# A norm weight applied to weight pieces on GpSimd, and its RMS factor applied to the products, in a two-layer decoder kernel

## The chip, the cores and the metric

The kernel runs on one core of a Trainium2 chip. The metric is the device time of one execution in microseconds (us). A core has five engines with instruction queues of their own, which the profile calls PE (TensorE, the matrix engine; PEld is its loading of stationary operands), DVE (VectorE), ACT (ScalarE), POOL (GpSimd) and SP (SyncE, which here only issues DMAs). Each engine works off its queue in order and waits where an instruction's operands aren't there yet.

## The reference

The input is x, 512 tokens of 2048 features in float32. Two layers follow each other. Each normalizes its input, mixes it, normalizes the result and adds it to the residual stream:

```python
def rms_norm(x, w):
    xf = x.astype(jnp.float32)
    y = xf * lax.rsqrt(jnp.mean(xf * xf, axis=-1, keepdims=True) + EPS)
    return (y * w.astype(jnp.float32)).astype(x.dtype)
...
    for layer in range(DEPTH):
        h = rms_norm(x, norm_pre[layer])
        ...
        x = x + rms_norm(y, norm_post[layer])
```

The even layer (layer 1 in the text) has gated linear recurrence heads and a gated MLP. The odd layer (layer 2) is a latent attention; its head is what matters here:

```python
    z = h @ w_in
    cq, ckv, kpe, gate = split_sizes(z, [C_Q_RANK, C_KV_RANK, C_ROPE, C_WIDTH])
    q = (rms_norm(cq, q_norm) @ w_qb).reshape(bsz, T, C_HEADS, C_QK)
    kv = (rms_norm(ckv, kv_norm) @ w_kvb).reshape(bsz, T, C_HEADS, C_NOPE + C_V)
    ...
    return (o * jax.nn.silu(gate)) @ w_out
```

`w_in` of the odd layer is 2048 x 3136: 512 columns for cq, 512 for ckv, 64 for the rotary key kpe, 2048 for the gate. EPS is 1e-6.

## The kernel before

The 512 tokens are four tiles of 128 (NT = 4), the 2048 features 16 blocks of 128 (KD = 16). Every float32 product is made of three matmuls in a reduced float32 format: each operand is split into a high part (a cast) and a low part (the operand minus its high part), and high x high, high x low and low x high are summed in PSUM. `tok_steps` (L209 to L211) does so with the activations stationary and 128 tokens in the partitions of the output, `feat_steps` (L214 to L216) with the weights stationary and 128 features in the partitions.

**Weights** come in pieces of 128 x 1024 numbers (512 KB). `fetch` issues the DMA on SP (L150) into `raw`, which has three buffers. `wload` splits the piece: ACT casts it into `whi` (L168), DVE makes `wlo` (L169). `piece(n)` prepares up to piece n + 3 (AHEAD). The pieces follow each other in one list, `plan`. A "stack" piece (the rotary key) writes high and low parts side by side (L162, L163).

**Activations** of a layer's input projection stand in R: 16 feature blocks, each as a high and a low tile of 128 features x 512 tokens. To get there, a tile of 128 tokens x 2048 features is transposed on TensorE in four groups of 512 features (L297; four 128 x 128 transposes into one PSUM bank `tp`), and each group is split from PSUM into R by ACT (L279) and DVE (L280). There are two `tp` banks in turn, so the third transpose of a tile needs the bank that the first one's two splits have read.

**The border of the two layers.** Layer 1 ends with `out_proj` ("eo"): 2048 output features in chunks of 512, 512, 512, 256 and 256. The last chunk runs tile by tile: 48 matmuls per token tile, then `last_evac` for this tile: squares on ACT (L673), weight of the post-norm on DVE (L674), sum of squares (L679), RMS factor `yrs` on POOL (`rstd_of`, L271 and L272), and four residual adds on DVE (L683), each 128 x 512: Wa = Wa * yrs + residual. Then `finish0` stores the tile (L710, four DMAs) and starts `pre_norm` of layer 2 for it: squares on ACT (L286), sum on DVE (L288), factor `prs` on POOL, and, put off by some ticks, four steps of one scaling on DVE (L292: B = Wa * prs * weight row) and one transpose (L297) with its two splits. `tick()` counts pieces in the matmul loops; `at(DEFER + c // 2, ...)` places the steps that many ticks on, so that they fall between matmuls of the following work. Layer 2 then runs `low_rank("cq")` (eight pieces; the first four tile by tile), the rotary key (one piece), `low_rank("ckv")` (eight pieces) and the gate (`proj_feat` for eight chunks of four pieces; `gate_evac`, L790 to L793, makes silu of each PSUM bank). In `low_rank`, each output row is normalized again with a factor `lrs` over its 512 features.

What sets the order on each engine: the kernel's Python code emits instructions, and the framework's scheduler then puts them into the five in-order queues and places the semaphores. So the order is fixed before the kernel runs, and an instruction that waits holds up all that stand behind it in its queue.

Of the kernel before, what the change touches and what calls it, by code (L numbers as in the profile page):

```python
# [10 lines left out]
F32 = mybir.dt.float32  # L11
# [7 lines left out]
P = 128  # L19
T = 512  # L20
NT = T // P
D = 2048
# [22 lines left out]
def trunk_kernel(ctx, tc, x, positions, norm_pre, norm_post, ev_w_in, ev_lb_logits, ev_a_onorm,  # L45
# [17 lines left out]
    def tp_bank():  # L63
        return ptp.tile([P, 512], F32, name="tp", tag="tp")
# [25 lines left out]
    def row_bc(dst, src_row):  # L90
        nc.sync.dma_start(out=dst, in_=src_row.partition_broadcast(P))
# [12 lines left out]
    mhalf = const.tile([P, 8], F32, name="mhalf")  # L104
    nc.gpsimd.memset(mhalf, -0.5)

    pk = const.tile([18, P], F32, name="pk")
    nc.sync.dma_start(out=pk[0:16, :], in_=ev_lb_logits.rearrange("l (h p) -> (l h) p", p=P))
    nc.sync.dma_start(out=pk[16:17, :], in_=ev_a_onorm)
    nc.sync.dma_start(out=pk[17:18, :], in_=inv_freq)  # L110

    cols = const.tile([P, 18], F32, name="cols")
    lb = const.tile([P, 8], F32, name="lb")
    oml = const.tile([P, 8], F32, name="oml")

    def setup_cols():
        tp = tp_bank()
        nc.tensor.transpose(tp[:, 0:18], pk, ident[0:18, 0:18])
        nc.scalar.copy(cols, tp[:, 0:18])
        e = sm.tile([P, 4, 8], F32, name="lbt", bufs=1)  # L120
        l0, l1 = cols[:, 0:8], cols[:, 8:16]
        nc.vector.tensor_tensor(e[:, 0], l0, l1, ALU.max)
        nc.vector.tensor_tensor(e[:, 1], l0, e[:, 0], ALU.subtract)
        nc.vector.tensor_tensor(e[:, 2], l1, e[:, 0], ALU.subtract)
        nc.scalar.activation(e[:, 1:3], e[:, 1:3], AF.Exp)
        nc.vector.tensor_tensor(e[:, 3], e[:, 1], e[:, 2], ALU.add)
        nc.vector.reciprocal(e[:, 3], e[:, 3])
        nc.vector.tensor_tensor(lb, e[:, 1], e[:, 3], ALU.mult)
        nc.vector.tensor_scalar(oml, lb, -1.0, 1.0, ALU.mult, ALU.add)
# [2 lines left out]
    def wview(w):  # L132
        return w.rearrange("(k p) c -> p k c", p=P)

    plan, ready, issued = [], {}, [0]
    AHEAD = 3
    DEFER = 6

    def plan_chunk(wv, c0, ncol, nk_all, nk, cuts=None):
        first = len(plan)  # L140
        for k in range(0, nk_all, nk):
            plan.append((wv[:, k:k + nk, c0:c0 + ncol], nk, ncol, cuts))
        return first

# [8 lines left out]
    def wload(i):  # L153
        _, nk, nco, cuts = plan[i]
        n = nk * nco
        if i not in fetched:
            fetch(i)
        raw = fetched.pop(i)
        if cuts == "stack":
            rv = raw[:, 0:n].rearrange("p (k c) -> p k c", k=nk)  # L160
            st = low_rank_act()[:, 8:12, :].rearrange("p a (k c) -> p (a k) c", c=P)
            nc.scalar.copy(st[:, :, 0:64], rv)  # L162
            nc.vector.tensor_tensor(st[:, :, 64:128], rv, st[:, :, 0:64].bitcast(F32), ALU.subtract)  # L163
            return st, None
# [104 lines left out]
    def rstd_of(ss, n, ncols, name, bufs=2):  # L269
        r = sm.tile([P, ncols], F32, name=name, bufs=bufs)  # L270
        nc.gpsimd.tensor_scalar(r, ss, 1.0 / n, EPS, ALU.mult, ALU.add)  # L271
        nc.gpsimd.tensor_tensor(r, r, mhalf[:, 0:ncols], ALU.pow)  # L272
        return r
# [62 lines left out]

    plan_out("eo", ev_w_out[0])
    for c in range(2):
        pl["cq", c] = plan_chunk(ow, CQ + 256 * c, 256, KD, 4)
    pl["kpe"] = plan_chunk(ow, KPE, 64, KD, KD, "stack")  # L340
    pl["ckv"] = plan_chunk(ow, CKV, 512, KD, 2)
    for c in range(8):
        pl["gate", c] = plan_chunk(ow, GATE + 256 * c, 256, KD, 4)
    for p in range(8):
        pl["q", p] = plan_chunk(qv, p * 384, 384, 4, 2, cuts_q)
        pl["kv", p] = plan_chunk(kvv, p * 512, 512, 4, 2)
# [307 lines left out]
    def out_proj(Wy, name, wpost_row, resid_t, junk, finish, early=KD, hook=None):  # L654
# [47 lines left out]
        proj_tok(pl[name, 3], 256, r_act, KD, lambda i, ps: evac(i, ps, 1536, 3))  # L702
        proj_tok(pl[name, 4], 256, r_act, KD, last_evac, tile_major=True)

    def finish0(i, ch):
        if i == 0:
            for c in range(4):
                row_bc(B[:, 4 + c, :], norm_pre[1, c * 512:(c + 1) * 512])
        for c in range(4):
            nc.sync.dma_start(out=x1_t[i][:, c * 512:(c + 1) * 512], in_=ch[c])  # L710
        pre_norm(i, ch, [B[:, 4 + c, :] for c in range(4)],
                 [B[:, 8 + 4 * (i % 2) + c, :] for c in range(4)], G[:, 8, :], DEFER)

    out_proj(W, "eo", norm_post[0], x_t, G[:, 8, :], finish0)

# [6 lines left out]
    def low_rank(name, wbc, rows, dst, first):  # L722
        ss = sm.tile([P, 4, 2], F32, name="lss")

        def evac(i, ps, half):
            n = ps.shape[-1]
            nc.scalar.activation(G[:, 8, 0:n], ps, AF.Square, accum_out=ss[:, i, half:half + 1])
            nc.vector.tensor_tensor(rows[i][:, half * 256:half * 256 + n], ps,
                                    wbc[:, half * 256:half * 256 + n], ALU.mult)

# [5 lines left out]
        else:  # L736
            proj_tok(pl[name], 512, r_act, KD, lambda i, ps: evac(i, ps, 0))
            s1 = ss[:, :, 0]
        r = rstd_of(s1, 512, 4, "lrs")
        def flip(i):  # L740
            tp = tp_bank()
            for j in range(4):
# [16 lines left out]
    def rope_half(dst, src_ps, src_sb, sw, n):  # L759
# [4 lines left out]
        nc.gpsimd.tensor_tensor(sw[0:n], sw[0:n], sinT[0:n], ALU.mult)  # L764
        nc.vector.tensor_tensor(dst[0:n], dst[0:n], sw[0:n], ALU.add)


    kps = mm_bank()
    stk, _ = piece(pl["kpe"])
# [244 lines left out]
```

## Time and profile before

| | us |
|---|---|
| median of 3 runs | 1601.81 (1601.14 to 1602.43) |
| the profiled execution | 1602.72 |
| its span, first to last instruction | 1601.0 |
| DVE, residual adds of layer 1 (L683), one of 128 x 512 | 0.747 (median of 16) |
| mean granted TensorE clock | 0.998 |

One execution was profiled, and it lies 0.9 us above the median of the runs. Durations are taken from it. In rows of the timeline the first number is the start in us from the start of the span, the second the duration; a bracket gives the idle time of the engine ahead of the instruction and what ended it. In rows of groups stand busy time, mean ns of one instruction, and idle time ahead with what ended most of it. `out<-in` gives the tiles by name, `raw`, `whi`, `wlo` for weights, `Wa` for the residual stream of layer 1's end, `B` for scaled rows, `R` for split activations, `G` for the residual loaded from memory.

### The profile page before, as it was taken

What the parts mean: (1) busy time and instruction counts of PE and PEld (TensorE: products, weight loads), DVE (VectorE), ACT (ScalarE), POOL (GpSimd) and SP (SyncE); (2) the same over time, 40 slices, a digit from 0 to 9 for tenths busy, and PEclk for the clock granted to TensorE, in tenths of its full rate; (3) what the DMA queues carried; (4) which work ended last, traced back from release to release, by engine and by line L of the source; (5) the groups of instructions that cost most, each with busy time, mean ns of one, the idle gap of its engine ahead of it and who ended that gap; (6) DMA issues with size and microseconds to landing.
All of it is one profiled execution on the core that took longest, in us unless ns stands there. A gap on an engine that the chain in (4) does not pass through costs nothing. (4 is left out here: it accounts for less than half of the span.)

```text
span 1601.0 us, 20791 instructions
## 1 busy us (share of the span) xinstructions
PE 1574.7 (98%) x8417; PEld 1359.2 (85%) x8417; DVE 752.5 (47%) x1346; ACT 534.6 (33%) x928; POOL 96.6 (6%) x145
## 2 busy tenths in 40 slices
PE   6999999999999999999999999999999999999997
PEld 5888888898888888888889988888889888988887
DVE  7653455535444224352225743232266767762224
ACT  6422322222222222232224433222265555642221
POOL 1000000000014004000001000000000000000000
PEclk9999999999999999999999999999999999999999
DMA  6432232223333333343325523333221221233224
GB/s 214 123 93 79 86 98 80 80 79 99 92 100 119 100 102 94 99 145 100 111 93 160 168 69 105 92 93 99 86 74 56 70 60 60 93 106 105 93 93 158
DMA packets 124299, 161.03 MB, mean 101 GB/s; under 512 B 7830, under 2 KB 86696, under 8 KB 124200
## 3 DMA queue, kind: packets, MB, share of 16 engines
q1 hardware_dynamic: 124204, 159.71, 32.1%
q8 instruction: 66, 1.08, 0.3%
q14 instruction: 29, 0.24, 0.0%
HBM read 151.30 MB, written 8.39 MB: 100 GB/s over the span
## 5 line engine op out<-in xcount | busy, mean ns | idle before, releaser
L169 DVE TENSOR_TENSOR wlo<-raw,whi 128x1024 fp32r<-128x1024 f32 x240 | 297.0, 1238 | 635.9 <-ACT whi L168 619.9
L168 ACT CAST whi<-raw 128x1024 fp32r<-128x1024 f32 x240 | 252.2, 1052 | 768.3 <-PE mm L211 338.9
L209 PE MATMUL mm<-whi,R 128*128 128x512 f32 (+1 forms) x1152 | 397.5, 345 | 0.0
L210 PE MATMUL mm<-wlo,R 128*128 128x512 f32 (+1 forms) x1152 | 395.8, 344 | 1.2 <-DVE wlo L169 1.2
L211 PE MATMUL mm<-whi,R 128*128 128x512 f32 (+1 forms) x1152 | 395.8, 344 | 0.0
L214 PE MATMUL mm<-R,whi 128*128 128x512 f32 x832 | 326.0, 392 | 0.0
L216 PE MATMUL mm<-R,wlo 128*128 128x512 f32 x832 | 324.0, 389 | 0.0
L215 PE MATMUL mm<-R,whi 128*128 128x512 f32 x832 | 323.9, 389 | 0.0
L210 PEld LDWEIGHTS mm<-wlo,R 128*128 128x128 f32 x1152 | 219.2, 190 | 26.3 <-DVE wlo L169 1.7
L211 PEld LDWEIGHTS mm<-whi,R 128*128 128x128 f32 x1152 | 219.1, 190 | 25.1
L209 PEld LDWEIGHTS mm<-whi,R 128*128 128x128 f32 x1152 | 219.2, 190 | 24.7 <-ACT R L279 0.2
L216 PEld LDWEIGHTS mm<-R,wlo 128*128 128x128 f32 x832 | 156.2, 188 | 32.8
L214 PEld LDWEIGHTS mm<-R,whi 128*128 128x128 f32 x832 | 156.2, 188 | 32.1
L215 PEld LDWEIGHTS mm<-R,whi 128*128 128x128 f32 x832 | 156.3, 188 | 31.8
L214 PE MATMUL mm<-Wc,whi 128*128 128x512 f32 x160 | 62.9, 393 | 0.0
L216 PE MATMUL mm<-Wc,wlo 128*128 128x512 f32 x160 | 62.6, 391 | 0.0
L215 PE MATMUL mm<-Wc,whi 128*128 128x512 f32 x160 | 62.4, 390 | 0.0
L280 DVE TENSOR_TENSOR R<-mm,R 128x512 fp32r<-128x512 f32 x48 | 32.9, 686 | 27.5 <-ACT R L279 27.5
L280 DVE TENSOR_TENSOR R<-tp,R 128x512 fp32r<-128x512 f32 x64 | 42.1, 684 | 4.0 <-ACT R L279 3.7
L279 ACT CAST R<-tp 128x512 fp32r<-128x512 f32 x64 | 35.9, 587 | 18.9 <-PE tp L297 17.0
L904 ACT ACTIVATE G<-sc,nm 128x512 f32<-128x512 f32 (+2 forms) x48 | 26.1, 546 | 41.2 <-DVE nm L903 41.2
L279 ACT CAST R<-mm 128x512 fp32r<-128x512 f32 x48 | 28.2, 587 | 31.8 <-PE mm L211 18.3
(245 smaller groups left out, 1653.7 us busy)
## 6 DMA issues: line engine op xcount, KB each, us to landing
raw<-in_ev_w_in_dram SPq DMA_DIRECT2D x112, 512.0 KB, 3.6
raw<-in_od_w_in_dram SPq DMA_DIRECT2D x49, 512.0 KB, 3.8
raw<-in_ev_w_out_dram SPq DMA_DIRECT2D x32, 512.0 KB, 3.6
raw<-in_od_w_out_dram SPq DMA_DIRECT2D x32, 512.0 KB, 3.5
raw<-in_od_w_kvb_dram SPq DMA_DIRECT2D x16, 512.0 KB, 3.5
raw<-in_od_w_qb_dram SPq DMA_DIRECT2D x16, 384.0 KB, 3.3
Wa<-in_x_dram SPq DMA_DIRECT2D x16, 256.0 KB, 5.7
G<-in_x_dram SPq DMA_DIRECT2D x16, 256.0 KB, 5.0
```

The lines of the kernel that those rows point to most:

```text
L168: nc.scalar.copy(hi[:, 0:n], raw[:, 0:n])
L169: nc.vector.tensor_tensor(lo[:, 0:n], raw[:, 0:n], hi[:, 0:n].bitcast(F32), ALU.subtract)
L209: nc.tensor.matmul(o, hh[:, sl], wh, start=first, stop=False, skip_group_check=True)
L210: nc.tensor.matmul(o, hh[:, sl], wl, start=False, stop=False, skip_group_check=True)
L211: nc.tensor.matmul(o, hl[:, sl], wh, start=False, stop=last, skip_group_check=True)
L214: nc.tensor.matmul(ps, hi, hh, start=first, stop=False)
L215: nc.tensor.matmul(ps, hi, hl, start=False, stop=False)
L216: nc.tensor.matmul(ps, lo, hh, start=False, stop=last)
L279: nc.scalar.copy(dst_hi, src)
L280: nc.vector.tensor_tensor(dst_lo, src, dst_hi.bitcast(F32), ALU.subtract)
L904: nc.scalar.activation(pv[j], sp[j], AF.Exp, bias=nm[:, j:j + 1], scale=C_SCALE, accum_out=su[:, j:j + 1])
```

## The change

The pre-norm of layer 2 is h = x * rn * w, with a factor rn for each token and a weight w for each feature. Before, both are applied to x ahead of its transposes. The change applies w to the rows of `w_in` and rn to the products.

- The 16 feature blocks of `norm_pre[1]` are brought into `cols` as 16 columns (one more small DMA at the start; the transpose in `setup_cols` takes 34 rows in place of 18).
- The 49 pieces of `w_in` (cq 8, kpe 1, ckv 8, gate 32) are marked in `norm_k`. In `wload`, POOL multiplies such a piece in place in `raw`, before the cast and the subtraction, by the column of its feature block, broadcast along the row.
- The four row broadcasts of `norm_pre[1]` and the 16 scalings (L292) of layer 2 are gone. The transposes take the residual stream Wa itself, one tick earlier (DEFER is 5).
- `factor()` makes rn of a tile three ticks after its first transposes: squares on ACT, a sum on DVE, three small operations on POOL. It also keeps EPS * (mean square + EPS), which takes the place of EPS in the factor `lrs` of cq and ckv, where rn cancels otherwise.
- `spread_rn1` puts rn of all tokens into each partition (four matmuls against the identity, one copy on ACT). The rotary key and each gate bank are multiplied by it: one more DVE operation on kz, and one on each of the 16 gate banks, in PSUM.

```diff
--- before.py
+++ after.py
@@ -104,19 +104,20 @@
     mhalf = const.tile([P, 8], F32, name="mhalf")
     nc.gpsimd.memset(mhalf, -0.5)
 
-    pk = const.tile([18, P], F32, name="pk")
+    pk = const.tile([34, P], F32, name="pk")
     nc.sync.dma_start(out=pk[0:16, :], in_=ev_lb_logits.rearrange("l (h p) -> (l h) p", p=P))
     nc.sync.dma_start(out=pk[16:17, :], in_=ev_a_onorm)
     nc.sync.dma_start(out=pk[17:18, :], in_=inv_freq)
-
-    cols = const.tile([P, 18], F32, name="cols")
+    nc.sync.dma_start(out=pk[18:34, :], in_=norm_pre[1].rearrange("(k p) -> k p", p=P))
+
+    cols = const.tile([P, 34], F32, name="cols")
     lb = const.tile([P, 8], F32, name="lb")
     oml = const.tile([P, 8], F32, name="oml")
 
     def setup_cols():
         tp = tp_bank()
-        nc.tensor.transpose(tp[:, 0:18], pk, ident[0:18, 0:18])
-        nc.scalar.copy(cols, tp[:, 0:18])
+        nc.tensor.transpose(tp[:, 0:34], pk, ident[0:34, 0:34])
+        nc.scalar.copy(cols, tp[:, 0:34])
         e = sm.tile([P, 4, 8], F32, name="lbt", bufs=1)
         l0, l1 = cols[:, 0:8], cols[:, 8:16]
         nc.vector.tensor_tensor(e[:, 0], l0, l1, ALU.max)
@@ -132,13 +133,15 @@
     def wview(w):
         return w.rearrange("(k p) c -> p k c", p=P)
 
-    plan, ready, issued = [], {}, [0]
+    plan, ready, issued, norm_k = [], {}, [0], {}
     AHEAD = 3
-    DEFER = 6
-
-    def plan_chunk(wv, c0, ncol, nk_all, nk, cuts=None):
+    DEFER = 5
+
+    def plan_chunk(wv, c0, ncol, nk_all, nk, cuts=None, normed=False):
         first = len(plan)
         for k in range(0, nk_all, nk):
+            if normed:
+                norm_k[len(plan)] = k
             plan.append((wv[:, k:k + nk, c0:c0 + ncol], nk, ncol, cuts))
         return first
 
@@ -156,6 +159,10 @@
         if i not in fetched:
             fetch(i)
         raw = fetched.pop(i)
+        if i in norm_k:
+            rv = raw[:, 0:n].rearrange("p (k c) -> p k c", k=nk)
+            nw = cols[:, 18 + norm_k[i]:18 + norm_k[i] + nk].unsqueeze(2).broadcast_to([P, nk, nco])
+            nc.gpsimd.tensor_tensor(rv, rv, nw, ALU.mult)
         if cuts == "stack":
             rv = raw[:, 0:n].rearrange("p (k c) -> p k c", k=nk)
             st = low_rank_act()[:, 8:12, :].rearrange("p a (k c) -> p (a k) c", c=P)
@@ -336,11 +343,11 @@
 
     plan_out("eo", ev_w_out[0])
     for c in range(2):
-        pl["cq", c] = plan_chunk(ow, CQ + 256 * c, 256, KD, 4)
-    pl["kpe"] = plan_chunk(ow, KPE, 64, KD, KD, "stack")
-    pl["ckv"] = plan_chunk(ow, CKV, 512, KD, 2)
+        pl["cq", c] = plan_chunk(ow, CQ + 256 * c, 256, KD, 4, normed=True)
+    pl["kpe"] = plan_chunk(ow, KPE, 64, KD, KD, "stack", normed=True)
+    pl["ckv"] = plan_chunk(ow, CKV, 512, KD, 2, normed=True)
     for c in range(8):
-        pl["gate", c] = plan_chunk(ow, GATE + 256 * c, 256, KD, 4)
+        pl["gate", c] = plan_chunk(ow, GATE + 256 * c, 256, KD, 4, normed=True)
     for p in range(8):
         pl["q", p] = plan_chunk(qv, p * 384, 384, 4, 2, cuts_q)
         pl["kv", p] = plan_chunk(kvv, p * 512, 512, 4, 2)
@@ -702,14 +709,44 @@
         proj_tok(pl[name, 3], 256, r_act, KD, lambda i, ps: evac(i, ps, 1536, 3))
         proj_tok(pl[name, 4], 256, r_act, KD, last_evac, tile_major=True)
 
+
+
+    rms1 = const.tile([P, 3, 4], F32, name="rms1")
+    rn1, eps_rn1 = rms1[:, 0], rms1[:, 1]
+    rb1 = const.tile([P, 512], F32, name="rb")
+
     def finish0(i, ch):
-        if i == 0:
-            for c in range(4):
-                row_bc(B[:, 4 + c, :], norm_pre[1, c * 512:(c + 1) * 512])
         for c in range(4):
             nc.sync.dma_start(out=x1_t[i][:, c * 512:(c + 1) * 512], in_=ch[c])
-        pre_norm(i, ch, [B[:, 4 + c, :] for c in range(4)],
-                 [B[:, 8 + 4 * (i % 2) + c, :] for c in range(4)], G[:, 8, :], DEFER)
+
+        def flip(c):
+            tp = tp_bank()
+            for j in range(4):
+                nc.tensor.transpose(tp[:, j * P:(j + 1) * P], ch[c][:, j * P:(j + 1) * P], ident)
+            sl = slice(i * P, (i + 1) * P)
+            split_into(R[:, 8 * c:8 * c + 8:2, sl], R[:, 8 * c + 1:8 * c + 8:2, sl],
+                       tp.rearrange("p (j t) -> p j t", j=4))
+
+        def factor():
+            ss = sm.tile([P, 4], F32, name="pss")
+            for c in range(4):
+                nc.scalar.activation(G[:, 8, :], ch[c], AF.Square, scale=D ** -0.5, accum_out=ss[:, c:c + 1])
+            s1 = rms1[:, 2, i:i + 1]
+            nc.vector.tensor_reduce(s1, ss, AX.X, ALU.add)
+            nc.gpsimd.tensor_scalar(s1, s1, EPS, None, ALU.add)
+            nc.gpsimd.tensor_scalar(eps_rn1[:, i:i + 1], s1, EPS, None, ALU.mult)
+            nc.gpsimd.tensor_tensor(rn1[:, i:i + 1], s1, mhalf[:, 0:1], ALU.pow)
+
+        for c in range(4):
+            at(DEFER + c // 2, lambda c=c: flip(c))
+        at(DEFER + 3, factor)
+
+    def spread_rn1():
+        tp = tp_bank()
+        for i in range(NT):
+            nc.tensor.matmul(tp[:, i * P:(i + 1) * P], rn1[:, i:i + 1].broadcast_to([P, P]), ident,
+                             start=True, stop=True)
+        nc.scalar.copy(rb1, tp)
 
     out_proj(W, "eo", norm_post[0], x_t, G[:, 8, :], finish0)
 
@@ -724,7 +761,7 @@
 
         def evac(i, ps, half):
             n = ps.shape[-1]
-            nc.scalar.activation(G[:, 8, 0:n], ps, AF.Square, accum_out=ss[:, i, half:half + 1])
+            nc.scalar.activation(G[:, 8, 0:n], ps, AF.Square, scale=512 ** -0.5, accum_out=ss[:, i, half:half + 1])
             nc.vector.tensor_tensor(rows[i][:, half * 256:half * 256 + n], ps,
                                     wbc[:, half * 256:half * 256 + n], ALU.mult)
 
@@ -736,7 +773,10 @@
         else:
             proj_tok(pl[name], 512, r_act, KD, lambda i, ps: evac(i, ps, 0))
             s1 = ss[:, :, 0]
-        r = rstd_of(s1, 512, 4, "lrs")
+        r = sm.tile([P, 4], F32, name="lrs")
+        nc.gpsimd.tensor_tensor(r, s1, eps_rn1, ALU.add)
+        nc.gpsimd.tensor_tensor(r, r, mhalf[:, 0:4], ALU.pow)
+
         def flip(i):
             tp = tp_bank()
             for j in range(4):
@@ -763,6 +803,8 @@
         nc.vector.tensor_tensor(dst[0:n], src_sb[0:n], cosT[0:n], ALU.mult)
         nc.gpsimd.tensor_tensor(sw[0:n], sw[0:n], sinT[0:n], ALU.mult)
         nc.vector.tensor_tensor(dst[0:n], dst[0:n], sw[0:n], ALU.add)
+
+    spread_rn1()
 
 
     kps = mm_bank()
@@ -776,6 +818,7 @@
     kz = B[:, 2, :]
     nc.scalar.copy(kz[0:64], kps[64:128])
     nc.vector.tensor_tensor(kz[0:64], kps[0:64], kz[0:64], ALU.add)
+    nc.vector.tensor_tensor(kz[0:64], kz[0:64], rb1[0:64], ALU.mult)
     rope_half(B[:, 3, :], kz, kz, B[:, 4, :], 64)
     KS1, KS2 = KS[:, 0, :], KS[:, 1, :]
     nc.scalar.copy(KS1[0:64], B[0:64, 3, :])
@@ -789,6 +832,7 @@
     for c in range(8):
         def gate_evac(m, ps, c=c):
             g = B[:, 2 * c + m, :]
+            nc.vector.tensor_tensor(ps, ps, rb1, ALU.mult)
             nc.scalar.activation(g, ps, AF.Sigmoid)
             nc.vector.tensor_tensor(g, ps, g, ALU.mult)
 
```

The scheduler moves some instructions besides. POOL, at the border, before: the factors of tiles 2 and 3, `yrs` for the post-norm and `prs` for the pre-norm (numbers are buffer numbers).

```order
L271 TENSOR_SCALAR yrs_6204<-ys1_6202 128x1
L272 TENSOR_TENSOR yrs_6204<-yrs_6204,mhalf_95 128x1
L271 TENSOR_SCALAR prs_6222<-ps1_6220 128x1
L272 TENSOR_TENSOR prs_6222<-prs_6222,mhalf_95 128x1
L271 TENSOR_SCALAR yrs_6309<-ys1_6307 128x1
L272 TENSOR_TENSOR yrs_6309<-yrs_6309,mhalf_95 128x1
L271 TENSOR_SCALAR prs_6327<-ps1_6325 128x1
L272 TENSOR_TENSOR prs_6327<-prs_6327,mhalf_95 128x1
```

The same place of POOL in the changed kernel, from `yrs` of tile 2 on: `raw_6325` is the fourth piece of cq (piece 3, counted from 0), `raw_6332`, `raw_6339` and `raw_6346` are pieces 4, 5 and 6.

```order
L278 TENSOR_SCALAR yrs_6191<-ys1_6189 128x1
L279 TENSOR_TENSOR yrs_6191<-yrs_6191,mhalf_95 128x1
L165 TENSOR_TENSOR raw_6325<-raw_6325,cols_102 128x1024
L736 TENSOR_SCALAR rms1_4908<-rms1_4908 128x1
L737 TENSOR_SCALAR rms1_4908<-rms1_4908 128x1
L738 TENSOR_TENSOR rms1_4908<-rms1_4908,mhalf_95 128x1
L165 TENSOR_TENSOR raw_6332<-raw_6332,cols_102 128x1024
L278 TENSOR_SCALAR yrs_6291<-ys1_6289 128x1
L279 TENSOR_TENSOR yrs_6291<-yrs_6291,mhalf_95 128x1
L165 TENSOR_TENSOR raw_6339<-raw_6339,cols_102 128x1024
L165 TENSOR_TENSOR raw_6346<-raw_6346,cols_102 128x1024
```

The factor of tile 3 (`yrs_6291`) now stands behind the multiply of piece 4, and the multiplies of pieces 5 and 6 stand right behind it. The multiplies of pieces 0 to 2 stand ahead of all `yrs`.

DVE, before, from the end of tile 3's matmuls on. `tp_6266` and `tp_6274` are tile 1's third and fourth transposes; tile 2's are not begun, since they wait for their scalings with `prs_6222`, which stand behind.

```order
L674 TENSOR_TENSOR Wa_80<-mm_5937,B_77 128x256
L679 TENSOR_REDUCE ys1_6307<-yss_4907 128x1
L169 TENSOR_TENSOR wlo_6342<-raw_6339,whi_6341 128x1024
L280 TENSOR_TENSOR R_76<-tp_6266,R_76 128x4x128
L280 TENSOR_TENSOR R_76<-tp_6274,R_76 128x4x128
L683 SCALAR_TENSOR_TENSOR Wa_80<-Wa_80,yrs_6309,G_78 128x512 x4
L292 SCALAR_TENSOR_TENSOR B_77<-Wa_80,prs_6222,B_77 128x512 x2
```

DVE, in the changed kernel, at the same place (L681 was L674, L690 was L683, L176 was L169, L287 was L280; `tp_6302` and `tp_6309` are tile 2's first two transposes):

```order
L681 TENSOR_TENSOR Wa_80<-mm_5940,B_77 128x256
L686 TENSOR_REDUCE ys1_6289<-yss_4910 128x1
L176 TENSOR_TENSOR wlo_6329<-raw_6325,whi_6328 128x1024
L690 SCALAR_TENSOR_TENSOR Wa_80<-Wa_80,yrs_6291,G_78 128x512 x4
L287 TENSOR_TENSOR R_76<-tp_6302,R_76 128x4x128
L287 TENSOR_TENSOR R_76<-tp_6309,R_76 128x4x128
```

The scalings are gone, and the transposes stand earlier against the residual adds: at tile 3's adds the changed kernel is about two transposes (half a tile) ahead of before. The lo halves of tile 2's first two transposes stand right behind the adds of tile 3. In the same way those of tile 1 stand behind tile 2's adds, and those of tile 0 behind tile 1's (in both kernels).

## The prediction

> **What bounds the kernel now.** I read the page first: busy times, the chain that ended last, then the two costliest groups of weight work.
>
> ```profile
> PE 1574.7 (98%) x8417; PEld 1359.2 (85%) x8417; DVE 752.5 (47%) x1346; ACT 534.6 (33%) x928; POOL 96.6 (6%) x145
> PE 44%; DVE 2%; DMA 0%; POOL 0%; issue 0%; ACT 0%; DVEq 0%; POOLq 0%; SPq 0%; ACTq 0%
> L169 DVE TENSOR_TENSOR wlo<-raw,whi 128x1024 fp32r<-128x1024 f32 x240 | 297.0, 1238 | 635.9 <-ACT whi L168 619.9
> L168 ACT CAST whi<-raw 128x1024 fp32r<-128x1024 f32 x240 | 252.2, 1052 | 768.3 <-PE mm L211 338.9
> ```
>
> TensorE is busy 98% of the span. DVE is under half busy, POOL idles. So freeing DVE or loading POOL is worth nothing by itself: only TensorE's own instructions and its waits count. Next, TensorE's waits by releaser, and the two 40 us stretches (start:end, length, then PE busy) around the border of the two layers, where the change works.
>
> ```profile
> PE tp L297 <- DVE B L292: 14.6, 6, 12.1
> PE tp L297 <- DVE R L280: 1.4, 1, 1.4
> 840.00:880.00 40.00, 37.71 (x310) 36.77 (x310) 23.61 (x39) 18.61 (x46) 4.59 (x10) 1.00 0.53 155
> 880.00:920.00 40.00, 39.47 (x328) 38.73 (x327) 28.95 (x43) 19.83 (x40) 3.26 (x6) 1.00 0.56 168
> ```
>
> The 14.6 us of the first row are mostly the kernel's start (12.1 in one wait). At the border TensorE is idle 40.00 − 37.71 + 40.00 − 39.47 = 2.8 us; busy time counts each matmul to its end, so the time lost between starts is somewhat more. The timeline shows where; its columns are start, duration, instruction, and the idle time ahead in brackets.
>
> ```profile
> 844.87 0.28 PE L209 MATMUL mm<-whi,R 128*128 128x256 f32 x1
> 844.99 0.28 PE L210 MATMUL mm<-wlo,R 128*128 128x256 f32 x1
> 863.11 0.28 PE L211 MATMUL mm<-whi,R 128*128 128x256 f32 x1
> 864.17 0.66 PE L297 MATMUL tp<-ident,B 128*128 128x128 f32 x4 [0.79 <-DVE B L292]
> 868.32 0.28 PE L210 MATMUL mm<-wlo,R 128*128 128x256 f32 x1
> 869.96 0.55 PE L297 MATMUL tp<-ident,B 128*128 128x128 f32 x3 [1.36 <-DVE R L280]
> 882.76 0.28 PE L209 MATMUL mm<-whi,R 128*128 128x256 f32 x1
> 883.52 0.41 PE L297 MATMUL tp<-ident,B 128*128 128x128 f32 x2 [0.48 <-DVE B L292]
> ```
>
> Undisturbed, a matmul of 256 columns follows the last after 844.99 − 844.87 = 0.12 us. The three pairs are 1.06, 1.64 and 0.76 us apart, so they lose 0.94, 1.52 and 0.64 us. With some smaller gaps my estimate is 3.9 us in all. That is everything the change can win here.
>
> **What it removes.** The 16 scalings of layer 2, and their two waits (0.94, 0.64). Group rows of DVE over 840 to 905 us:
>
> ```profile
> L292 DVE SCALAR_TENSOR_TENSOR B<-Wa,prs,B 128x512 f32<-128x512 f32 x16 | 11.6, 745 | 1.2 <-POOL prs L272 1.2
> L683 DVE SCALAR_TENSOR_TENSOR Wa<-Wa,yrs,G 128x512 f32<-128x512 f32 x16 | 11.1, 748 | 2.5 <-POOL yrs L272 2.5
> L280 DVE TENSOR_TENSOR R<-tp,R 128x512 fp32r<-128x512 f32 x16 | 10.7, 685 | 0.7 <-ACT R L279 0.6
> ```
>
> That is 11.6 us of DVE, and four row broadcasts on SP. A transpose now needs the residual add (L683) alone. The third wait (868, two banks of tp, freed by the lo half L280) isn't removed, and it is the one that I expect to grow.
>
> **What it adds: 49 multiplies on POOL.** No row of before has this operation. Nearest is the rotary POOL product, half as large, with its minimum, median and maximum:
>
> ```profile
> L618 POOL TENSOR_TENSOR Wa<-Wa,B 128x512 f32<-128x512 f32 x16 | 26.9, 1720 | 1.1 <-DVE Wa L612 1.1
> L618 POOL TENSOR_TENSOR Wa<-Wa,B x16: 1282/1304/2277, 483.3 to 629.6; 128x512 f32<-128x512 f32 x16
> L169 DVE TENSOR_TENSOR wlo<-raw,whi x240: 1160/1225/2306, 13.9 to 1571.1; 128x1024 fp32r<-128x1024 f32 x120
> 483.33 1.29 POOL L618 TENSOR_TENSOR Wa<-Wa,B 128x512 f32<-128x512 f32 x1 [0.53 <-DVE Wa L612]
> 484.13 1.58 DVE L169 TENSOR_TENSOR wlo<-raw,whi 128x1024 fp32r<-128x1024 f32 x1
> ```
>
> Twice 1.28 is 2.56 us for 128x1024; the mean gives 3.44, with waits in it. I take 2.56. A fixed share could make it a little less; 2.4 and 3.44 are the ends kept. The wlo that starts at 484.13 ends at 485.71, 1.09 us after the POOL instruction's end at 484.62: most of its 1.225 us came after it. So the two took turns. A second case is on the border itself, the other way about: a tiny POOL power takes 1.58 us against a wlo, and 0.56 alone.
>
> ```profile
> 884.36 1.21 DVE L169 TENSOR_TENSOR wlo<-raw,whi 128x1024 fp32r<-128x1024 f32 x1
> 884.40 1.58 POOL L272 TENSOR_TENSOR prs<-prs,mhalf 128x1 f32<-128x1 f32 x1
> 857.65 0.56 POOL L272 TENSOR_TENSOR yrs<-yrs,mhalf 128x1 f32<-128x1 f32 x1
> 856.29 0.39 ACT L673 ACTIVATE G<-mm 128x256 f32<-128x256 f32 x1 [3.98 <-PE mm L211]
> 858.24 1.42 DVE L683 SCALAR_TENSOR_TENSOR Wa<-Wa,yrs,G 128x512 f32<-128x512 f32 x2 [0.95 <-POOL yrs L272]
> ```
>
> So I let DVE operations with two operands in SBUF (wlo, residual add) and POOL's multiply exclude each other. For the residual add no row of before shows it: its ends are 0 and a full multiply each, and I take the latter, since both of its big operands lie in SBUF as wlo's do. The Trainium skill, "SBUF — State Buffer", section "Who interferes with whom", states the same as an exclusive lock on a port pair that VectorE and GpSimd share, for VectorE operations with two SBUF inputs; the wlo row (1.58 against 1.225) agrees, no run here shows it for the residual add. Without that rule the residual add would be free, and the sum 5.0 us smaller: the first rival below.
>
> In the gate phase a piece feeds 24 matmuls of 512 columns, about 24 × 2 × 0.12 = 5.8 us of TensorE; a multiply and a wlo in turn take 2.56 + 1.225 = 3.8, and pieces are prepared three ahead. I cost those 32 multiplies, and the ckv and kpe ones, at nothing: TensorE's matmuls of three pieces cover them. If a multiply took 3.44, 4.7 us would still fit. The low-rank factors of cq and ckv queue behind one multiply each, and their transposes come two pieces later; cq's is tight (0.3 us in hand by my replay, a loss of about 1 us if it isn't). The extra gate product (DVE, a PSUM bank in place, nearest the L280 row's 0.69) delays bank release by 0.69 us; the second bank pair covers it. The start gets one more small DMA and a reshuffled queue: ±1 us, taken as 0.
>
> **The border step by step.** Times are on before's clock. From a tile's end to its residual add (L673 at 856.29, L683 at 858.24) 1.95 us pass; four adds take 2.74 us.
>
> ```profile
> raw<-in_od_w_in_dram SPq DMA_DIRECT2D x49, 512.0 KB, 3.8
> 866.56 2.74 DVE L683 SCALAR_TENSOR_TENSOR Wa<-Wa,yrs,G 128x512 f32<-128x512 f32 x4 [0.72 <-POOL yrs L272]
> 869.22 1.28 DVE L280 TENSOR_TENSOR R<-tp,R 128x512 fp32r<-128x512 f32 x2
> 877.23 0.38 SPq L150 DMA_DIRECT2D raw<-in_od_w_in_dram  x1
> 881.83 1.05 ACT L168 CAST whi<-raw 128x1024 fp32r<-128x1024 f32 x1 [0.59 <-DMA raw<-in_od_w_in_dram]
> ```
>
> In the order of after, the lo halves of a tile's first two transposes stand on DVE behind the whole residual add of the next tile (before, only tile 0's did), and its third transpose needs their tp bank.
> - Tile 0: its first two transposes no longer wait (0.94 won). TensorE reaches the third 32 matmuls later, at 866.65. DVE does tile 1's adds from 865.2 to 867.95, then the lo half: 868.6. **Lost: 1.95.**
> - Tile 1: tile 2's adds run 875.1 to 877.85, one wlo to 879.0, the lo half to 879.65; TensorE was there at 877.6. **Lost: 2.05.**
> - Piece 3: its buffer is freed by that wlo (879.0), and it lands 3.8 us later (the page's median; 4.6 in the rows above), 882.8. Now the multiply comes ahead of the cast: 885.4, then whi 886.4. At about that moment POOL begins piece 4's multiply, so wlo of piece 3 waits for it to end (888.7) and is done at 889.9. TensorE wants it at 887.1, 20 matmuls into the piece. **Lost: 2.8.**
> - Tile 2: on POOL, tile 3's factor stands behind piece 4's multiply, and behind the factor stand the multiplies of pieces 5 and 6 without a gap. The factor is there at 890.4; four adds of 0.69 and two multiplies of 2.56 in turn end at 890.4 + 2.75 + 5.1 − 0.25 (overlap of starts) = 898.0; the lo half is done at 898.65. TensorE reached the third transpose at 892.05. **Lost: 6.6.**
>
> By then DVE has caught up; tile 3's transposes come tight, with nothing queued ahead of them.
>
> Lost after: 1.95 + 2.05 + 2.8 + 6.6 = 13.4; before 3.9; so +9.5. Spreading the factors adds four transposes' worth of matmuls, 4 × 0.12 = +0.5 us at most of TensorE. A long idle might also slow the matmuls for a while; the only slow pace in before is at its start:
>
> ```profile
> 18.39 0.41 PE L209 MATMUL mm<-whi,R 128*128 128x256 f32 x1
> 18.61 0.41 PE L210 MATMUL mm<-wlo,R 128*128 128x256 f32 x1
> ```
>
> There the pace is 0.22 us in place of 0.12, for some 3 us: 0 to 1.4 us here. After the 1.5 us idle at 868 the pace was full, the nearest case, so I take 0. The Trainium skill, "TensorE: Matmul & The Clock Gate", Part 1 "What's actually happening", has a half clock follow an idle window of about 3.4 us; the starting rows agree with a slow pace, no run here shows it in mid-kernel, and the sum by it would be 1.4 us more.
>
> Sum: 1602.7 us (the profiled execution) + 9.5 + 0.5 = 1612.7; this execution lies 0.9 us over the median, so **1611.8** for the median.
>
> **The rivals.** The bound between no change and a change is 0.2%, 3.2 us, about what a measurement of this kernel can tell: 1598.6 and 1605.0.
> - *Multiplies don't hold up residual adds.* For it: no row of before shows that they do. Against: wlo. The adds of tile 3 then end at 893.1, not 898.0, and the last loss falls by 5: 1611.8 − 5.0 = 1606.8, and 1604.0 where wlo of piece 3 also slips in ahead of the multiply (2.8 less). 0.22, of which 0.12 within 0.2%.
> - *The border's waits go* (the other side). Place: the lo halves of tiles 0 to 2. It decides if DVE, rid of 11.6 us, comes to them before TensorE needs the third transpose, that is, if residual adds start 2 us earlier than worked out, and piece 3 lands with the multiply still hidden. Against: the order puts the lo halves behind the adds. 1601.8 − 3.9 + 0.5 = 1598.4. Half removed: 1600. 0.16, half of it faster.
> - *POOL's multiply is 3.44 us.* Piece 3 and tile 2 lose four times 0.88: 1615.3. 0.13.
> - My forecast: 0.49.
>
> **The numbers.** The range goes from 1598.0 (second rival) to 1617.7 (3.44, the slow pace and the start's 1 us). Faster 0.09; same 0.08 + 0.12 = 0.20; slower the rest, 0.71.
>
> **What the profile after would show.** Right: TensorE idles at four places between 860 and 900, released by the lo half of R twice about 2 us, by wlo of piece 3, and longest by the lo half after tile 3's adds; L165 at about 2.56 us alone; residual adds of tile 3 stretched to 3 us. Wrong: adds at 0.75 beside a running multiply (first rival); third transposes without idle time (second); TensorE idle in the gate phase, which I count as covered; multiplies far from 2.56; a start moved by over 1 us.

## The result, and the profile after

| | median, us | runs | range |
|---|---|---|---|
| before | 1602.33 | 6 | 1601.14 to 1602.81 |
| changed | 1612.54 | 6 | 1611.70 to 1613.71 |

The ratio is 1.0064, with a 95% interval of 1.0054 to 1.0074: the change costs about 10 us. The profiled execution took 1612.93 us, its span is 1610.9.

First come the line of the page with the changed kernel's busy time per engine, then TensorE's waits by releaser (total, times, longest), then the stretches around the border of the layers (start:end, length, then PE, PEld, DVE, ACT and POOL busy, granted clock, DMA share, GB/s).

```profile
PE 1576.7 (98%) x8425; PEld 1361.3 (85%) x8425; DVE 783.0 (49%) x1347; ACT 534.2 (33%) x929; POOL 194.3 (12%) x198
```

```profile
PE tp L725 <- DVE R L287: 9.1, 3, 7.0
PE mm L216 <- ACT whi L175: 1.5, 2, 1.0
PE mm L217 <- DVE wlo L176: 1.3, 2, 0.9
```

```profile
840.00:880.00 40.00, 37.90 (x317) 37.50 (x316) 22.98 (x36) 18.52 (x47) 9.49 (x12) 1.00 0.60 183
880.00:920.00 40.00, 31.62 (x240) 31.01 (x239) 19.36 (x27) 15.54 (x35) 13.18 (x16) 0.87 0.29 89
960.00:1000.00 40.00, 40.00 (x178) 33.15 (x177) 14.35 (x10) 10.76 (x16) 15.10 (x10) 1.00 0.32 93
```

TensorE's own work grew by 2.0 us at most (busy 1574.7 to 1576.7). Its waits for the scalings at the border are gone; a wait of the transposes for the lo half of R, 1.4 us in all before, is 9.1 now, 7.0 of it in one place. From 880 to 920 us TensorE is busy 31.62 us where it was 39.47, and the granted clock, 1.00 in the other rows, is 0.87. In the gate phase (960 to 1000), with a multiply for each piece, TensorE has no idle time: there the multiplies cost nothing.

The border on TensorE, from the timeline of the changed kernel (start, duration, instruction, idle time ahead and its end):

```profile
865.75 0.28 PE L217 MATMUL mm<-wlo,R 128*128 128x256 f32 x1
867.24 0.33 PE L725 MATMUL tp<-ident,Wa 128*128 128x128 f32 x1 [1.22 <-DVE R L287]
...
875.80 0.28 PE L217 MATMUL mm<-wlo,R 128*128 128x256 f32 x1
876.97 0.30 PE L725 MATMUL tp<-ident,Wa 128*128 128x128 f32 x1 [0.89 <-DVE R L287]
...
883.77 0.28 PE L218 MATMUL mm<-whi,R 128*128 128x256 f32 x1
884.59 0.38 PE L216 MATMUL mm<-whi,R 128*128 128x256 f32 x1 [0.55 <-ACT whi L175]
885.85 0.39 PE L217 MATMUL mm<-wlo,R 128*128 128x256 f32 x1 [0.88 <-DVE wlo L176]
...
887.99 0.28 PE L216 MATMUL mm<-whi,R 128*128 128x256 f32 x1
895.23 1.11 PE L725 MATMUL tp<-ident,Wa 128*128 128x128 f32 x4 [6.96 <-DVE R L287]
...
897.42 0.41 PE L216 MATMUL mm<-whi,R 128*128 128x256 f32 x1
897.64 0.41 PE L217 MATMUL mm<-wlo,R 128*128 128x256 f32 x1
```

With 0.12 us from matmul to matmul taken off, the third transpose of tile 0 loses 867.24 - 865.75 - 0.12 = 1.37 us, that of tile 1 1.05, piece 3's cast 0.70 and its wlo 1.14, and the third transpose of tile 2 loses 7.12. Behind it matmuls come every 897.64 - 897.42 = 0.22 us. From 895.23 to 901.34 TensorE started 14 matmuls and 16 transposes, which take 3.4 us at the full pace (0.12 and 0.11 each): 2.7 us more are lost.

What held tile 2's transpose stands in the timelines of POOL and DVE:

```profile
881.57 1.90 POOL L165 TENSOR_TENSOR raw<-raw,cols 128x1024 f32<-128x1024 f32 x1 [9.26 <-DMA raw<-in_od_w_in_dram]
883.55 0.24 POOL L736 TENSOR_SCALAR rms<-rms 128x1 f32<-128x1 f32 x1
883.87 0.23 POOL L737 TENSOR_SCALAR rms<-rms 128x1 f32<-128x1 f32 x1
884.15 0.57 POOL L738 TENSOR_TENSOR rms<-rms,mhalf 128x1 f32<-128x1 f32 x1
884.69 2.87 POOL L165 TENSOR_TENSOR raw<-raw,cols 128x1024 f32<-128x1024 f32 x1
887.64 0.19 POOL L278 TENSOR_SCALAR yrs<-ys 128x1 f32<-128x1 f32 x1
887.91 0.56 POOL L279 TENSOR_TENSOR yrs<-yrs,mhalf 128x1 f32<-128x1 f32 x1
888.44 1.89 POOL L165 TENSOR_TENSOR raw<-raw,cols 128x1024 f32<-128x1024 f32 x1
890.81 1.90 POOL L165 TENSOR_TENSOR raw<-raw,cols 128x1024 f32<-128x1024 f32 x1 [0.48 <-DMA raw<-in_od_w_in_dram]
```

```profile
872.34 2.74 DVE L690 SCALAR_TENSOR_TENSOR Wa<-Wa,yrs,G 128x512 f32<-128x512 f32 x4 [0.95 <-POOL yrs L279]
...
884.57 1.22 DVE L176 TENSOR_TENSOR wlo<-raw,whi 128x1024 fp32r<-128x1024 f32 x1 [3.16 <-ACT whi L175]
888.50 6.07 DVE L690 SCALAR_TENSOR_TENSOR Wa<-Wa,yrs,G 128x512 f32<-128x512 f32 x4 [2.71 <-POOL yrs L279]
894.50 1.27 DVE L287 TENSOR_TENSOR R<-tp,R 128x512 fp32r<-128x512 f32 x2
```

Tile 3's factor (L278, L279) starts at 887.64, behind the multiplies of pieces 3 and 4. Its four residual adds begin at 888.50, 0.06 us after piece 5's multiply has begun, and take 6.07 us where tile 2's took 2.74; that multiply and piece 6's, 1.9 us each, run beside them. The lo half comes right behind, at 894.50, and TensorE goes on at 895.23.

### The profile page after: what moved, and what is told of

The parts are those of the page before. It is cut to its first block, busy times and chain, and to the rows that moved or that the text cites. A ratio compares the mean times of both kernels' runs of the same rounds, so it can differ in the third digit from the quotient of the medians.

```text
span 1610.9 us, 20872 instructions
## 1 busy us (share of the span) xinstructions
PE 1576.7 (98%) x8425; PEld 1361.3 (85%) x8425; DVE 783.0 (49%) x1347; ACT 534.2 (33%) x929; POOL 194.3 (12%) x198
## 4 chain that ended last, share of the span: by engine, by line
PE 94%; DVE 2%; DMA 1%; POOL 1%; issue 1%; ACT 0%; DVEq 0%; POOLq 0%; ACTq 0%
PE mm L221 14%; PE mm L223 14%; PE mm L222 14%; PE mm L217 13%; PE mm L218 13%; PE mm L216 13%; PE tp L959 1%; PE sc L222 1%; PE sc L223 1%; PE sc L221 1%; PE sc L497 1%; DVE Wa L690 1%; PE tp L972 1%; PE tp L971 1%; PE tp L970 1%
## 5 line engine op out<-in xcount | busy, mean ns | idle before, releaser
L176 DVE TENSOR_TENSOR wlo<-raw,whi 128x1024 fp32r<-128x1024 f32 x240 | 322.2, 1344 | 604.5 <-ACT whi L175 592.6
L165 POOL TENSOR_TENSOR raw<-raw,cols 128x1024 f32<-128x1024 f32 x49 | 99.1, 2023 | 377.5 <-DMA raw<-in_od_w_in_dram 360.4
L287 DVE TENSOR_TENSOR R<-mm,R 128x512 fp32r<-128x512 f32 x48 | 32.9, 686 | 27.8 <-ACT R L286 27.8
L287 DVE TENSOR_TENSOR R<-tp,R 128x512 fp32r<-128x512 f32 x64 | 41.7, 683 | 7.5 <-ACT R L286 7.2
```

The lines of the kernel that those rows point to most:

```text
L165: nc.gpsimd.tensor_tensor(rv, rv, nw, ALU.mult)
L176: nc.vector.tensor_tensor(lo[:, 0:n], raw[:, 0:n], hi[:, 0:n].bitcast(F32), ALU.subtract)
L287: nc.vector.tensor_tensor(dst_lo, src, dst_hi.bitcast(F32), ALU.subtract)
```

## The experiments

Each kernel was timed beside the kernel before on the same chip; "over before" is the difference of the two medians (15 to 27 runs of before in a group, medians 1601.4 to 1601.8 us). On the same footing the changed kernel stands 10.2 us over before.

### Taking the multiplies away, and nothing else

Three kinds of cost stand behind the 7.12 us: the factor's place on POOL behind piece 4, the multiplies beside the adds, and the plain order of DVE. Four kernels leave out multiplies; on the engines but POOL their instructions stand in the order of the changed kernel, but for one placement on TensorE and ACT in the first of them.

```diff
-        if i in norm_k:
+        if i in norm_k and i - pl["cq", 0] not in (4, 5, 6):
```

The set is all 49 pieces in the first run, then pieces 4 to 6 of cq, piece 4 alone, and pieces 5 and 6.

> The changed kernel without the 49 multiplies of weight pieces on POOL (the norm weight of layer 2 is left out); the order of every other instruction is that of the changed kernel. Theory (the multiplies hold up tile 3's residual adds and delay piece 3; the long wait that follows then brings a slow TensorE pace): the two waits of the third transposes of tiles 0 and 1 stay (about 1.4 and 1.1 us), the one of tile 2 falls from 7.1 to at most 1.5 us, tile 3's four adds take 2.74 us and not 6.07, no stretch of the border shows a granted clock under 0.99, and the time is 1601 to 1603 us. Rival (the order, with lo halves behind the next tile's adds, makes the wait, whatever POOL does): the wait of tile 2 stays over 4 us and the time over 1608.

> The changed kernel without the multiplies of pieces 4, 5 and 6 of cq (their norm weight is left out); every other instruction in the order of the changed kernel. Theory (it is these three, around tile 3's factor and adds): piece 3 stays as late as in the changed kernel (its cast and its wlo waited for, about 1.8 us together), tile 3's adds take 2.74 us, tile 2's third transpose waits at most 1.5 us, no slow pace: 1603 to 1605 us. Rival (piece 3, landing late and multiplied, delays all that follows, and the multiplies behind cost nothing more): over 1609 us.

> The changed kernel without the multiply of piece 4 alone (its norm weight is left out); all else in the order of the changed kernel. It takes the multiply away behind which tile 3's factor stands on POOL, and leaves those of pieces 5 and 6 beside tile 3's residual adds. Theory (adds and multiplies take turns): the factor is there 2 us earlier than in the changed kernel, the four adds still take about 6 us, tile 2's third transpose waits about 5 us, and a slow pace follows: 1608 to 1610.5 us. Rival (the factor's place in POOL's queue is the whole cost): adds in 2.74 us, wait under 2 us, 1605 us or less.

> The changed kernel without the multiplies of pieces 5 and 6 (their norm weight is left out); all else in the order of the changed kernel. The factor of tile 3 still stands behind piece 4's multiply; nothing on POOL runs beside the adds. Theory: adds in 2.74 us, tile 2's third transpose waits 7.1 - 3.3 = about 3.8 us, perhaps with a short slow pace: 1606 to 1609 us. Rival (the multiplies beside the adds cost nothing, since they overlap): over 1611 us.

| left out | median, us | over before | ratio, interval | adds of tile 3 | tile 2's wait |
|---|---|---|---|---|---|
| all | 1602.02 | 0.6 | 1.0003 (0.9994 to 1.0011) | 2.74 | 1.41 |
| 4, 5, 6 | 1604.78 | 3.4 | 1.0023 (1.0014 to 1.0031) | 2.74 | 1.81 |
| 4 | 1607.62 | 5.9 | 1.0036 (1.0023 to 1.0048) | 4.37 | 3.43 |
| 5, 6 | 1609.64 | 7.9 | 1.0045 (1.0032 to 1.0058) | 2.74 | 3.79 |
| none | 1612.54 | 10.2 | 1.0064 (1.0054 to 1.0074) | 6.07 | 7.12 |

The last two columns are the duration of L690 x4 and the gap before the third transpose less 0.12. The rows of DVE, in the table's order, without the last:

```profile
883.21 2.74 DVE L690 SCALAR_TENSOR_TENSOR Wa<-Wa,yrs,G 128x512 f32<-128x512 f32 x4 [1.37 <-POOL yrs L279]
```

```profile
886.55 2.74 DVE L690 SCALAR_TENSOR_TENSOR Wa<-Wa,yrs,G 128x512 f32<-128x512 f32 x4 [0.72 <-POOL yrs L279]
```

```profile
886.57 4.37 DVE L690 SCALAR_TENSOR_TENSOR Wa<-Wa,yrs,G 128x512 f32<-128x512 f32 x4 [0.72 <-POOL yrs L279]
```

```profile
887.83 2.74 DVE L690 SCALAR_TENSOR_TENSOR Wa<-Wa,yrs,G 128x512 f32<-128x512 f32 x4 [2.71 <-POOL yrs L279]
```

Without any multiply the kernel is as fast as before within what can be told, though the order of its other work is the changed one: the rival by which the order makes the long wait falls. Without pieces 4 to 6 tile 2's wait was 1.81 us, not at most 1.5: there the first POOL operation of tile 3's factor took 1.04 us in place of 0.19, beside the wlo of piece 3:

```profile
884.83 1.04 POOL L278 TENSOR_SCALAR yrs<-ys 128x1 f32<-128x1 f32 x1
```

```profile
884.60 1.23 DVE L176 TENSOR_TENSOR wlo<-raw,whi 128x1024 fp32r<-128x1024 f32 x1 [3.52 <-ACT whi L175]
```

The 2.8 us between these two kernels are about what their traces show: 1.06 and 1.14 us lost at piece 3's cast and wlo in the second, and 0.4 us more at each of two transposes. No run leaves out piece 3's multiply alone.

Pieces 4 to 6 make 10.2 - 3.4 = 6.8 us of the cost; the first of them (behind which the factor queues) and the other two (beside the adds) each account for a part, and neither rival that made one of them the whole cost holds. With piece 4 left out I had expected adds of about 6 us and 1608 to 1610.5 us. They took 4.37: piece 6 landed only after the adds, so one multiply stood beside them, not two.

```profile
886.50 1.90 POOL L165 TENSOR_TENSOR raw<-raw,cols 128x1024 f32<-128x1024 f32 x1
891.17 1.90 POOL L165 TENSOR_TENSOR raw<-raw,cols 128x1024 f32<-128x1024 f32 x1 [2.77 <-DMA raw<-in_od_w_in_dram]
```

One multiply beside the adds costs 4.37 - 2.74 = 1.63 us, two cost 3.33. With pieces 5 and 6 left out the wait was 3.79 us, as worked out ahead (3.8), but the time came out over the forecast (1609.64 against 1609 at most). The slow pace behind the wait was not short: from 891.23 to 897.16 TensorE started 14 matmuls and 16 transposes again, so it lost 5.93 - 3.44 = 2.5 us, and with piece 4 left out 1.6 us by the same count. One of the five runs without pieces 5 and 6 took 1606.17 us, the others 1609.25 to 1610.45; there is no trace of that run, so whether it went without the slow pace is open. How the pace hangs on the wait is told below.

### One tick later

```diff
-    DEFER = 5
+    DEFER = 6
```

> The changed kernel with the transposes put off by one tick more (DEFER 6, as before the change). The multiply of piece 4 then stands behind tile 3's factor, not ahead of it, but wlo of piece 3 behind tile 3's adds. Theory: the adds are still held up by the multiplies of pieces 4 and 5, and wlo of piece 3 comes late: 1607 to 1612 us. Rival (one tick less of deferral is what costs): as before the change, 1600 to 1604 us.

It took 1607.04 us (ratio 1.0035, 1.0023 to 1.0048), 5.6 over before, at the low end of what was expected. The factor of tile 3 now comes ahead of piece 4's multiply, but the adds still meet multiplies. Here one add stands alone in a row, the multiply beside it:

```profile
883.55 1.90 POOL L165 TENSOR_TENSOR raw<-raw,cols 128x1024 f32<-128x1024 f32 x1
```

```profile
883.62 2.38 DVE L690 SCALAR_TENSOR_TENSOR Wa<-Wa,yrs,G 128x512 f32<-128x512 f32 x1 [3.23 <-POOL yrs L279]
```

The add starts 0.07 us after the multiply and takes 2.38 us in place of 0.75: the multiply ends at 885.45, and the add 0.55 us later, at 886.00. So an add that comes second waits for all but the multiply's last moments. Before was DEFER 6 too; the rival that the one tick is what costs falls.

### The product on the gate banks

```diff
-            nc.vector.tensor_tensor(ps, ps, rb1, ALU.mult)
```

> The changed kernel without the product of the gate's banks with the RMS factor (the factor is left out of the gate). Theory (it lies beside TensorE's work): the time of the changed kernel, 1612.5 +- 1 us. Rival (16 products of about 0.7 us delay the release of banks): 2 us or more less.

1611.68 us (1611.04 to 1612.88), 9.9 over before against 10.2: the 16 products are hidden, as costed.

### The weight without POOL, and two mixtures

The weight can go into the split itself: ACT casts raw times the column, DVE subtracts.

```diff
+        if i in norm_k:
+            for k in range(nk):
+                ks = slice(k * nco, (k + 1) * nco)
+                w = cols[:, 18 + norm_k[i] + k:19 + norm_k[i] + k]
+                nc.scalar.activation(hi[:, ks], raw[:, ks], AF.Copy, scale=w)
+                nc.vector.scalar_tensor_tensor(lo[:, ks], raw[:, ks], w, hi[:, ks].bitcast(F32),
+                                               ALU.mult, ALU.subtract)
```

> The weight goes into the split itself in place of POOL: ACT casts raw times the column into whi, DVE makes wlo as raw times the column minus whi, in parts of one feature block each (4 of 256 columns or 2 of 512); only the rotary key's piece is multiplied on POOL. The order at the border differs somewhat. Theory: no multiply holds up the adds, so as without the multiplies, 1600 to 1603 us, though cast and subtraction in four parts cost some 0.4 us more each. Rival (ACT and DVE, with longer splits, now come late for TensorE in the border or the gate phase): over 1605 us.

1604.09 us (ratio 1.0017, 1.0007 to 1.0026). It does away with the long wait (the longest at the border is 1.4 us), but it is about 1 us above the range that I gave: neither side was right. The second kernel spaces a tile's transposes further apart:

```diff
-            at(DEFER + c // 2, lambda c=c: flip(c))
+            at(DEFER + 4 * (c // 2), lambda c=c: flip(c))
```

> As the kernel in which ACT and DVE apply the weight in the split, with a tile's third and fourth transposes put off by four ticks, not one, after the first two. TensorE then reaches tile 0's third transpose 48 matmuls after its first two (32 so far), and the lo halves are done: the first wait (0.9 us) goes, those of tiles 1 and 2 about halve: 1601 to 1603.5 us, 1 to 2 less than without the delay. Rival (the lo halves, now later, hold up the first matmuls of layer 2 or the next transposes by as much): the same 1604 us or more.

1603.73 us (ratio 1.0012, 1.0002 to 1.0021), between the two sides (1603.5 at most, 1604 or more). The wait of tile 0 is gone, as expected, but a later one grew to 1.95 us, and the gain (2.0 us over before in place of 2.7) is too small to tell from none. In both kernels the profiled execution (1602.94 and 1602.34 us) was faster than the median, so where their last 2 to 3 us over before go is left open.

The third and fourth kernels put the two together: POOL multiplies all pieces but 3 to 7 of cq, ACT and DVE weight those five, and the transposes are spaced by four ticks, with DEFER 6 and DEFER 4.

> POOL multiplies all pieces but 3 to 7 of cq, as in the changed kernel; those five are weighted by ACT and DVE in the split. A tile's first two transposes come one tick later (DEFER 6), the last two four ticks after them. Theory: no multiply stands beside tile 3's factor and adds; the lo halves have 48, 39 and 33 matmuls of time, so the border loses 2 to 4 us in all, against 4.6 before the change, and later multiplies are covered: 1600 to 1602.5 us, no more than 1 us from the kernel before. Rival (what remains is elsewhere, in the start and in the four matmuls that spread the factors): 1603 us or more, as with the weight in the split throughout.

> The same, but with a tile's first two transposes one tick earlier than in the changed kernel (DEFER 4), so that tile 0's first lo half is done ahead of tile 1's adds. Theory: the border loses 2 to 4 us here too, 1600 to 1602.5 us; where the first two transposes then wait for the adds themselves, 1 us more than the run beside it. Rival: 1603 us or more.

They took 1602.20 us (ratio 1.0004, 0.9995 to 1.0013) and 1601.03 us (0.9998, 0.9989 to 1.0007), against 1601.82 for before: 44 multiplies on POOL are there, and the loss is gone. (The transposes are spaced differently too, and no run separates the two.) With DEFER 6 one wait of 3.0 us was left, so the border lost more than I had expected; with DEFER 4 none is over 0.75. The stretches of the border in the last one:

```profile
840.00:880.00 40.00, 39.21 (x325) 38.45 (x325) 23.82 (x38) 18.99 (x47) 9.77 (x15) 1.00 0.59 181
880.00:920.00 40.00, 39.47 (x329) 39.08 (x330) 24.44 (x44) 21.96 (x53) 10.38 (x13) 1.00 0.48 138
```

TensorE is idle 0.79 + 0.53 = 1.3 us there, less than before (2.8). That didn't make a kernel that is measurably faster than before; it is some 11 us faster than the change as it was made.

## Why the prediction was right

The forecast was 1611.8 us, the time 1612.54; over before, 10.0 us were forecast and 10.2 measured. The mechanism is the one forecast: third transposes that wait for lo halves behind the next tile's adds, piece 3 late by its multiply, and tile 3's factor and adds held up by multiplies. But two terms were mis-sized, the waits by 2.0 us too much and the slow pace by 2.7 too little. That the total comes so near is in part luck.

| step | predicted, us | measured |
|---|---|---|
| tile 0, third transpose | 1.95 | 1.37 |
| tile 1, third transpose | 2.05 | 1.05 |
| piece 3, cast and wlo | 2.8 | 0.70 + 1.14 |
| tile 2, third transpose | 6.6 | 7.12 |
| sum of waits | 13.4 | 11.4 |
| slow pace after the long wait | 0 | 2.7 |

The 6.6 us for tile 2 is luck too. Its transpose began 3.4 us earlier than worked out (895.23 against 898.65), and TensorE had been ready 3.9 us earlier (888.11 against 892.05); the difference of the two came out nearly the same.

**The price of a multiply** was 2.56 us by the row of L618. The prediction calls it the rotary product; it is the scale and shift of layer 1's gated MLP, and its second operand is a row of 128 numbers repeated four times. The rotary product is another row of before, with two full operands, and takes as long:

```profile
L764 POOL TENSOR_TENSOR G<-G,sinT 128x512 f32<-128x512 f32 x8 | 10.4, 1302 | 386.7 <-ACT G L762 205.7 <-PE mm L215 181.0
```

The trace of the changed kernel gives 1.89 to 1.90 us for a multiply where nothing holds it up:

```profile
L165 POOL TENSOR_TENSOR raw<-raw,cols x49: 1888/1898/2881, 844.7 to 1139.2; 128x1024 f32<-128x1024 f32 x49
```

That lies below the lower end that I kept (2.4), and the rival of 3.44 us falls. Whether the broadcast column or the length makes a number cheaper, no run shows. The two multiplies beside tile 3's adds were costed at 5.1 - 0.25 = 4.85 us and cost 3.33.

**Waits of tiles 0 and 1.** The place was right, the size was not: the adds came 1.35 us (tile 1, 863.85 for 865.2) and 2.8 us (tile 2, 872.34 for 875.1) earlier than my replay had them. TensorE reached tile 1's third transpose 1.7 us earlier too (875.9 for 877.6), so only part of it is won. Why the adds came earlier than in the replay was not traced.

**Piece 3.** Its buffer came free 2.8 us earlier than worked out, but the piece took 5.3 us from issue (876.24) to the multiply's start, not 3.8. The turn was the other way: wlo of piece 3 started at 884.57, 0.12 us ahead of piece 4's multiply, and the multiply waited (2.87 us for 1.90). So wlo was not held up. The prediction's step "wlo of piece 3 waits for it to end" is wrong; the cost fell on POOL, and with it on tile 3's factor.

**Tile 3's adds.** The step on which most rested, that adds and multiplies exclude each other, was an assumption without a row; it is shown now, by the single add of 2.38 us and by the adds of 2.74, 4.37 and 6.07 us beside none, one and two multiplies. The rival that multiplies don't hold up the adds falls, and so does the one by which the border's waits go. The Trainium skill, "SBUF — State Buffer", section "Who interferes with whom", says that contention on the shared port pair is an exclusive lock, and that the order of issue decides who blocks; the trace agrees in both directions, with the add that waits (2.38 us) and the multiply that waits for a wlo (2.87).

**The slow pace** was taken at 0, from the 1.5 us idle before; that row was too short to tell. The next rows give the granted clock (third number from the end) in stretches of five kernels: without pieces 4 to 6, the mixture with DEFER 6, without piece 4, without 5 and 6, and the changed one. The gaps between two of TensorE's starts were 1.9, 3.1, 3.5, 3.9 and 7.2 us.

```profile
890.00:895.00 5.00, 5.00 (x44) 4.98 (x45) 3.61 (x8) 3.57 (x8) 2.04 (x6) 1.00 0.35 131
```

```profile
880.00:885.00 5.00, 2.20 (x20) 2.18 (x20) 3.39 (x6) 3.94 (x11) 0.00 (x0) 1.00 0.72 253
```

```profile
892.00:894.00 2.00, 2.00 (x11) 2.00 (x10) 1.22 (x4) 0.87 (x2) 1.77 (x4) 0.50 0.37 132
```

```profile
890.00:891.00 1.00, 0.00 (x0) 0.00 (x0) 1.00 (x2) 0.16 (x2) 0.00 (x0) 0.50 1.03 371
890.00:895.00 5.00, 3.77 (x18) 3.77 (x19) 3.55 (x7) 2.27 (x7) 1.02 (x3) 0.50 0.49 170
```

```profile
890.00:895.00 5.00, 0.00 (x0) 0.00 (x0) 5.00 (x5) 1.45 (x4) 2.23 (x2) 0.59 0.32 120
895.00:896.00 1.00, 0.77 (x5) 0.77 (x5) 1.00 (x4) 0.00 (x0) 0.07 (x1) 0.50 1.10 336
896.00:898.00 2.00, 2.00 (x11) 2.00 (x10) 0.86 (x2) 1.14 (x3) 0.96 (x3) 0.50 0.17 58
898.00:900.00 2.00, 2.00 (x12) 2.00 (x11) 0.85 (x2) 1.38 (x5) 0.23 (x1) 0.50 0.00 0
900.00:905.00 5.00, 5.00 (x40) 5.00 (x39) 2.51 (x4) 2.32 (x4) 0.80 (x2) 0.89 0.00 0
```

After 1.9 and 3.1 us the clock stays full. After 3.5 us or more it is 0.50 for a while, and work resumes at half pace; in the changed kernel it is back only after 900 us. The length alone does not decide it: without pieces 5 and 6 the clock stood at 0.50 at 890 us, only 2.7 us after TensorE's last start (887.32). The longest waits here were dearer than their length: the slow pace cost 1.6, 2.5 and 2.7 us behind the gaps of 3.5, 3.9 and 7.2. The Trainium skill, "TensorE: Matmul & The Clock Gate", Part 1 "What's actually happening", has a half clock after an idle window of about 3.4 us; the lengths of these five gaps agree, while the drop after 2.7 us came sooner. The rule, which the prediction gave beside the sum with a loss of 1.4 us, would have been the better choice, though the loss was 2.7.

**What was costed at nothing** held: in the gate phase TensorE is busy 40.00 of 40.00 us, although wlo went from 1238 to 1344 ns on average over the 240 pieces, 25 us of DVE in all:

```profile
L176 DVE TENSOR_TENSOR wlo<-raw,whi 128x1024 fp32r<-128x1024 f32 x240 | 322.2, 1344 | 604.5 <-ACT whi L175 592.6
```

**The start** was taken as 0, within 1 us either way, and no run separates it. In the profiled executions the first row of L618 (L625 in the changed kernel) begins at 483.33 us before and at 482.69 after, 0.6 us earlier. With this, and with the prediction's estimates of 3.9 us lost before and 0.5 us for spreading the factors, the account closes: 11.4 + 2.7 - 3.9 + 0.5 - 0.6 = 10.1 us, where the two profiled executions are 10.2 us apart.

## What to carry to other kernels

An engine that is idle 94% of the time is not free to use: ask what stands behind the new work in its queue, and which other engine's instructions take turns with it. Here a kernel with 44 of the 49 multiplies is as fast as before, while three of the other five, next to a short chain that TensorE waited for, cost 7 us. Where a wait may grow to 3.5 us or more, add the slow restart to it (1.6 to 2.7 us here). A broadcast weight that must be applied on the way can ride in operations that run anyway (a scale in the cast, a fused multiply in the subtraction), and be left to the idle engine only where the chain is slack.

## What the runs showed of the hardware

- POOL's multiply of 128x1024 by a broadcast column takes 1.90 us, 1.85 ns for each column; with two full operands it took 1.30 us for 512 columns (L764), 2.5 ns for each.
- A DVE operation with two operands in SBUF and POOL's multiply go one after the other, whichever starts first: add second, 2.38 us for 0.75; multiply second, 2.87 us for 1.90, with starts 0.07 and 0.12 us apart. Even a POOL operation on 128x1 is held up beside a wlo: 1.04 us for 0.19, without pieces 4 to 6.
- TensorE's clock was granted in full after gaps of 1.9 and 3.1 us between starts, and at 0.50 after gaps of 3.5, 3.9 and 7.2 us.
